# Writing the C11 quarter of a Strassen product from inside the stage that computes P2

## The chip, the cores and the metric

The kernel runs on one core of one Trainium2 chip. The metric is device time in microseconds (us) of one execution. PE is TensorE, DVE is VectorE, ACT is ScalarE, POOL is GpSimd; SP is SyncE, which here only issues transfers. "Kept" tensors lie in the chip's DRAM.

## The reference

Each token has eight experts; the output is the sum of their products, weighted by a softmax over the experts.

```python
def reference(x, router_logits, expert_weights):   # (16,512,512), (16,512,8), (8,512,2048)
    probs = exp(router_logits - max); probs = probs / sum(probs)
    for e in range(8):
        output += probs[:, :, e:e+1] * np.matmul(x, expert_weights[e])
    return output                                   # (16,512,2048) float32
```

Scaling x by the probabilities first makes this one product: 8192 tokens, an inner dimension of 8 x 512 = 4096, and 2048 output columns.

## The kernel before

**Algebra.** That product is cut into 2 x 2 blocks (tokens, experts, output columns) and done with seven products in place of eight, as Strassen and Winograd do. P1 and P2 are two of the seven, and the output block C11 is P1 + P2. Some of the seven, P1 and P2 among them, are themselves cut in the same way, with seven inner products each. `sub_product` computes one of these.

**Stages.** The program runs, in this order: an early part that sets up the probabilities and the first rows; `sub_product(1, ...)` for P1; `sub_product(5, ...)`; `sub_product(2, ...)` for P2; `sub_product(4, ...)`; and the main phase (L598 to L731), a loop over 16 groups of rows `q` that computes the remaining products and puts the output together. Stages 1, 5 and 2 store their results in `kept[r]` in DRAM; stage 4 stores straight into the output. The main phase loads P1 (`m1`) and the result of stage 5 (`m5`) back through `load_kept`, and P2 in `c11` (L588), where DVE adds P1 and the result is stored to the output.

**Inside `sub_product`** (L367). The outer loop is over `d`, eight passes. A pass loads x and probabilities (`load_x`, `load_p`), multiplies them on DVE into four z tiles (`mul`) and makes four more by additions. The inner loop is over `u`, two halves of 128 tokens. A half does seven products of eight matmuls (128 x 128 by 128 x 512) into PSUM banks named "x", "b", "q" and "d". Three products accumulate onto a bank that already holds one. ACT copies results out (`keep`, L402) and DVE combines them (`put`, L407), giving four tiles of 128 x 512 float32 per half: (group of 256 rows, column half) = (0,0), (0,1), (1,1), (1,0). `to_kept` stores them from SP. Product 1 has a bank of its own until ACT has copied it (`r1`), and `r5` and `r2` are two more such copies.

**Weights on the side.** After each pass `next(prep)` advances a generator that prepares the weights of the next stage, inside `behind()` (L125), which holds what it issues behind the last noted instruction of each engine. In P2's stage it is `weights_of_t4` (L497): after each of passes 0 to 3 it asks for a set of weight blocks (two casting loads of 512 KB, and one or two loads of 1 MB), one pass later it combines them on DVE and stores two blocks of 1 MB, and then asks for the next. `load` (L158) lets a DVE memset of two columns precede the load, so POOL's load waits for DVE.

**Queues and order.** Weight loads, casts and most output stores are issued by POOL; x, probabilities, kept tensors and weight stores by SP. Each engine works through its own instructions in order. A scheduler chooses that order beforehand, by program order and by what it reckons to be ready; `tc.keep_in_program_order` pins an instruction to program order. `dve` (L114) pins where `pinned[0]` is true, and `act` is the same function. During the four `sub_product` stages nothing is pinned, and their ACT copies are issued without `act`.

**Buffers.** Tiles of 128 x 512 float32 come from 15 slots, which `share` (L78) deals out to uses: in a new share, each use gets the slots that have been untouched longest, and `h_tile` takes the slots of a use in rotation. P2's stage has `share(xs=3, r=4, o=8)`: three for fresh x, four for ACT's copies, eight for results. PSUM has 8 banks of 128 x 512 float32, taken in rotation.

Of the kernel before, what the change touches and what calls it, by code (L numbers as in the profile page):

```python
# [32 lines left out]
def kernel(  # L33
# [7 lines left out]
    nc = tc.nc  # L41
    P = 128
    f16 = mybir.dt.float16
    f32 = mybir.dt.float32
# [8 lines left out]
    NB = 512  # L53
# [24 lines left out]
    def share(**sizes):  # L78

        order = sorted(used, key=used.get)  # L80
        for use, n in sizes.items():
            places[use], order = [order[:n], 0], order[n:]
# [24 lines left out]
    last = {}  # L107

    pinned = [True]

    def note(i):
        last[i.ins.engine] = i.ins
# [3 lines left out]
        if pinned[0]:  # L116
            tc.keep_in_program_order(i)

    act = dve

    def tt(o, a, b, op):
        dve(nc.vector.tensor_tensor(out=o, in0=a, in1=b, op=op))  # L122
# [222 lines left out]
        return z.rearrange("p e c t -> p (e c) t")  # L345


    kept = {r: [dram.tile([2, HQ, NB], f32, name=f"kept{r}_{i}") for i in range(NI)] for r in (1, 2, 5)}

    def half(use="any"):  # L350
        return h_tile([P, NB], f32, use)
# [10 lines left out]
    def from_kept(r, i, u, n, use):  # L362
        t = half(use)
        sp(t, kept[r][i][n, ds(u * P, P), :])
        return t

    def sub_product(r, odd, first, w, prep, start=0, zs=None, rest=()):  # L367

        for d in range(start, NI // 2):
            if zs:  # L370
                (a11, a12), (a21, a22) = zs
                zs = None
            else:
                hs = [4 * d + odd, 4 * d + 2 + odd]
                xp = [(load_x(h), load_p(h, first)) for h in hs]
                a11, a12 = (mul(*xp[0], e0, 2, 0, HQ) for e0 in (0, 2))
                a21, a22 = (mul(*xp[1], e0, 2, 0, HQ) for e0 in (0, 2))

            def new(a, b, op):
                z = zpool.tile([P, K8, HQ], f16, name="z", tag="z")  # L380
                tt(z, a, b, op)
                return z
            s1 = new(a21, a22, ADD)
            s2 = new(s1, a11, SUB)
            s4 = new(a12, s2, SUB)
            tt(a21, a11, a21, SUB)
            for make in rest:
                make()
            rest = ()
            z = {1: a11, 2: a12, 3: s4, 4: a22, 5: s1, 6: s2, 7: a21}  # L390

            for u in range(HQ // P):
                banks = {}

                def prod(p, b, start=True):
                    if start:
                        banks[b] = bank()
                    for k in range(K8):
                        mm(banks[b], z[p][:, k, ds(u * P, P)], w[p][:, k, :], start and k == 0, k == K8 - 1)
                    return banks[b]  # L400

                def keep(ps):  # L402
                    t = half("r")
                    nc.scalar.copy(t, ps)  # L404
                    return t

                def put(t, n, a, b, op):  # L407
                    o = half("o")
                    tt(o, a, b, op)
                    to_kept(r, 2 * d + t, u, n, o)  # L410

                r1 = keep(prod(1, "x"))
                put(0, 0, prod(2, "b"), r1, ADD)
                r5 = keep(prod(5, "q"))
                r2 = keep(prod(6, "x", False))
                put(0, 1, prod(3, "q", False), r2, ADD)
                prod(7, "x", False)
                r3 = keep(banks["x"])
                put(1, 1, banks["x"], r5, ADD)
                put(1, 0, r3, prod(4, "d"), SUB)  # L420
            with behind():
                store_x()
                next(prep, None)
        for _ in prep:
            pass
# [44 lines left out]
    def weights_of_t1():  # L470
# [5 lines left out]
            store("t1", kn, b[kn])  # L476
        yield
        ready[5] = yield from inner_weights(b)
    pinned[0] = False
    share(xs=3, r=4, o=8)  # L480
    sub_product(1, 0, P1, w, weights_of_t1(), 1,
                [[z.rearrange("p e c t -> p (e c) t") for z in zz] for zz in z1], (sums[3], sums[2]))
# [14 lines left out]
    def weights_of_t4():  # L497
# [12 lines left out]
            tt(b[kn], b[kn], t2, SUB)  # L510
        yield
        ready[4] = yield from inner_weights(b)
    share(xs=3, r=4, o=8)
    sub_product(2, 0, P2, ready[2], weights_of_t4())


    w6, w7, w3 = {}, {}, {}
# [18 lines left out]
    class Rows:  # L536
# [48 lines left out]
            self.m1[tn] = from_kept(1, self.q, *tn, "m")  # L585
            self.m5[tn] = from_kept(5, self.q, *tn, "v")

        def c11(self, j):  # L588
            tn = QUARTERS[j]
            m2 = from_kept(2, self.q, *tn, "m")  # L590
            tt(m2, self.m1[tn], m2, ADD)
            self.put(0, 0, tn, m2)

        def put(self, odd, cols, tn, o, **how):
            queue = nc.sync if self.q == NI - 1 and not how else nc.gpsimd
            queue.dma_start(out=out_rows(self.q, odd, tn[0], cols, tn[1]), in_=o, **how)  # L596
# [4 lines left out]
            make(k)  # L601
    for j in range(2):
        rows.load_kept(j)
        rows.c11(j)
    pinned[0] = True
    o10 = None
    sums = inner_weights(w3)
    for q in range(NI):
# [14 lines left out]
        for j, tn in enumerate(QUARTERS):  # L623
            if j > 1:
                rows.load_kept(j)
            x = bank()
            act(nc.scalar.copy(x, rows.m1[tn]))  # L627
            if o10 and j == 0:
                o10()
            if j > 1 or q == 1:  # L630
                rows.c11(j)
            if j < 2:
                rows.s4(j)
            else:
                ahead("a11", j - 2)
            plain(x, 6, w6, tn, False)
            v = half("u")
            tt(v, x, rows.m5[tn], ADD)
            xs.append(x)
            vs.append(v)  # L640
# [30 lines left out]
        def early(j):  # L671
            if following:
                following.load_kept(j)
                if q:
                    following.c11(j)

        ahead("s3", 0)
        if q == 0:
# [81 lines left out]
```

## Time and profile before

The median of three runs is 1435.09 us (1434.97 to 1435.35). The profiled execution has a span of 1433.2 us and a granted clock of 0.999.

| stage | from to (us) | PE busy | DVE busy | ACT busy | POOL busy | DMA share |
|---|---|---|---|---|---|---|
| early part | 0 to 42.6 | 40.6 | 26.6 | 14.9 | 12.0 | 1.03 |
| P1 | 42.6 to 211.8 | 169.2 | 123.5 | 34.0 | 17.4 | 0.98 |
| stage 5 | 211.8 to 405.2 | 193.4 | 124.7 | 37.5 | 15.2 | 0.87 |
| P2 | 405.2 to 598.6 | 193.4 | 142.3 | 37.5 | 10.4 | 0.78 |
| stage 4 | 598.6 to 792.0 | 193.4 | 132.1 | 38.8 | 13.5 | 0.70 |
| main phase | 792.0 to 1429.2 | 637.0 | 479.2 | 110.1 | 152.6 | 0.75 |

All of it is in us but the last column, the mean busy share of the 16 DMA engines, which counts the packets of two queues side by side and so can be over 1. A stage is taken to end with its last matmuls. In lines of the profile, L122 is `tt`, L142 is `mm`, L133 is `sp`, L136 is `pool`, L404 is the copy in `keep` and L596 is the output store of the main phase; a row gives an engine, an operation, what it writes and reads, its count, its busy time and the mean of one in ns, and then the idle time ahead of it with what ended that.

### The profile page before, as it was taken

What the parts mean: (1) busy time and instruction counts of PE and PEld (TensorE: products, weight loads), DVE (VectorE), ACT (ScalarE), POOL (GpSimd) and SP (SyncE); (2) the same over time, 40 slices, a digit from 0 to 9 for tenths busy, and PEclk for the clock granted to TensorE, in tenths of its full rate; (3) what the DMA queues carried; (4) which work ended last, traced back from release to release, by engine and by line L of the source; (5) the groups of instructions that cost most, each with busy time, mean ns of one, the idle gap of its engine ahead of it and who ended that gap; (6) DMA issues with size and microseconds to landing.
All of it is one profiled execution on the core that took longest, in us unless ns stands there. A gap on an engine that the chain in (4) does not pass through costs nothing.

```text
span 1433.2 us, 18192 instructions
## 1 busy us (share of the span) xinstructions
PE 1427.0 (100%) x6661; PEld 649.4 (45%) x6661; DVE 1029.0 (72%) x1171; ACT 272.8 (19%) x475; POOL 221.0 (15%) x346
## 2 busy tenths in 40 slices
PE   9999999999999999999999999999999999999998
PEld 4444444444444444444444444444444444444443
DVE  5867585647686877766767687777777877877773
ACT  3211111111111111111111211111111111111111
POOL 3111100111001000001000122222222222222220
PEclk9999999999999999999999999999999999999999
DMA  9899967799839994368865967788777777778764
GB/s 194 188 231 252 274 168 198 180 250 271 216 134 311 344 355 162 130 186 223 217 249 195 308 199 231 235 239 235 231 217 228 207 217 212 228 234 242 220 198 103
DMA packets 194329, 319.44 MB, mean 223 GB/s; under 512 B 53824, under 2 KB 83008, under 8 KB 189632
## 3 DMA queue, kind: packets, MB, share of 16 engines
q1 hardware_dynamic: 137072, 202.92, 44.7%
q0 software_dynamic: 57168, 115.37, 34.7%
q8 instruction: 52, 0.85, 0.3%
q14 instruction: 37, 0.30, 0.1%
HBM read 180.65 MB, written 159.58 MB: 237 GB/s over the span
## 4 chain that ended last, share of the span: by engine, by line
PE 94%; DMA 3%; issue 1%; POOL 1%; DVE 0%; ACT 0%; SPq 0%; POOLq 0%; DVEq 0%; ACTq 0%
PE ps L142 94%; DMA h<-kept 1%; DMA w<-in_expert_weights_dram 1%; DMA out_dram<-h 1%; POOL out_dram L596 1%; POOL w L136 0%; DVE h L122 0%; DVE z L122 0%; ACT ps L627 0%; ACT ps L646 0%; SPq L133 0%; POOL ident L235 0%; POOLq L596 0%; DVEq L122 0%; POOLq L235 0%
## 5 line engine op out<-in xcount | busy, mean ns | idle before, releaser
L142 PE MATMUL ps<-w,z 128*128 128x512 f16 x6552 | 1415.6, 379 | 0.3 <-ACT ps L627 0.2
L142 PEld LDWEIGHTS <-z 128*128 128x128 f16 x6552 | 640.9, 98 | 772.5 <-issue 0.9
L122 DVE TENSOR_TENSOR h<-ps,h 128x512 f32<-128x512 f32 x389 | 267.5, 688 | 311.2 <-PE ps L142 104.6
L122 DVE TENSOR_TENSOR z<-xT,pT 128x2048 f16<-128x2048 f16 x248 | 299.2, 1217 | 30.9 <-PE ps L142 30.9
L122 DVE TENSOR_TENSOR z<-z 128x2048 f16<-128x2048 f16 x280 | 303.5, 1107 | 7.7 <-DVE z L122 0.5
L404 ACT COPY h<-ps 128x512 f32<-128x512 f32 x248 | 145.3, 586 | 601.6 <-PE ps L142 598.3
L596 POOL DMA_DIRECT2D out_dram<-h x244 | 153.7, 664 | 533.4 <-DVE h L122 323.0
L122 DVE TENSOR_TENSOR w<-w 128x4096 f16<-128x4096 f16 x36 | 82.2, 2284 | 2.4 <-DMA w<-wdt 1.6
L663 ACT COPY h<-ps 128x512 f32<-128x512 f32 x64 | 37.4, 585 | 178.3 <-PE ps L142 175.4
L136 POOL DMA_DIRECT2D h<-in_x_dram x32 | 22.7, 709 | 283.6 <-DMA xT<-h 234.2
L122 DVE TENSOR_TENSOR h<-h 128x512 f32<-128x512 f32 (+1 forms) x67 | 46.0, 686 | 21.4 <-DMA h<-kept 21.2
L122 DVE TENSOR_TENSOR h<-h,ps 128x512 f32<-128x512 f32 x77 | 52.4, 681 | 11.4 <-PE ps L142 10.6
L136 POOL DMA_DIRECT2D w<-in_expert_weights_dram x41 | 30.7, 765 | 168.6 <-issue 77.0
L646 ACT ACTIVATE ps<-h 128x512 f32<-128x512 f32 x34 | 20.5, 602 | 160.3 <-DVE h L122 160.3
L627 ACT COPY ps<-h 128x512 f32<-128x512 f32 x64 | 35.6, 593 | 40.3 <-DMA h<-kept 31.9
L136 POOL DMA_DIRECT2D w<-wd x12 | 6.5, 542 | 188.2 <-DVE w L161 115.1
L723 ACT COPY h<-ps 128x512 f32<-128x512 f32 x15 | 8.8, 585 | 120.7 <-PE ps L142 120.7
L260 DVE CAST z<-ps 128x512 f16<-128x512 f32 x16 | 10.2, 684 | 10.4 <-PE ps L142 10.3
L712 ACT COPY h<-ps 128x512 f32<-128x512 f32 x15 | 8.8, 588 | 16.5 <-PE ps L142 16.5
L258 ACT CAST z<-ps 128x512 f16<-128x512 f32 x16 | 8.7, 589 | 16.2 <-PE ps L142 16.0
L142 PE MATMUL ps<-h,w 128*128 128x128 f16 (+1 forms) x96 | 8.5, 237 | 0.5 <-DVE lg L300 0.3
L142 PEld LDWEIGHTS <-w 128*128 128x128 f16 x96 | 6.9, 98 | 2.9 <-issue 0.7
(31 smaller groups left out, 35.0 us busy)
## 6 DMA issues: line engine op xcount, KB each, us to landing
out_dram<-h POOLq DMA_DIRECT2D x244, 256.0 KB, 5.0
kept<-h SPq DMA_DIRECT2D x192, 256.0 KB, 4.5
h<-kept SPq DMA_DIRECT2D x192, 256.0 KB, 4.8
pT<-p_dram SPq DMA_DIRECT2D x124, 256.0 KB, 5.3
w<-in_expert_weights_dram POOLq DMA_DIRECT2D x39, 512.0 KB, 12.4
out_dram<-h SPq DMA_DIRECT2D x76, 256.0 KB, 3.4
xT<-x SPq DMA_DIRECT2D x60, 256.0 KB, 3.0
w<-wd POOLq DMA_DIRECT2D x12, 1024.0 KB, 9.9
```

What stands on the lines that cost most here:

```text
L122: dve(nc.vector.tensor_tensor(out=o, in0=a, in1=b, op=op))
L136: note(nc.gpsimd.dma_start(out=o, in_=i))
L142: nc.tensor.matmul(ps, z, w, start=start, stop=stop, skip_group_check=True)
L258: act(nc.scalar.copy(o, ps))
L260: dve(nc.vector.tensor_copy(o, ps))
L404: nc.scalar.copy(t, ps)
L596: queue.dma_start(out=out_rows(self.q, odd, tn[0], cols, tn[1]), in_=o, **how)
L627: act(nc.scalar.copy(x, rows.m1[tn]))
L646: act(nc.scalar.mul(banks[b], v, scale))
L663: act(nc.scalar.copy(c21, x))
L712: act(nc.scalar.copy(r1, x))
L723: act(nc.scalar.copy(r3, x))
```

## The change

P2's stage gets the argument `prev=1`. It then loads the tiles of P1 itself, half a pass ahead (`load_prev`, four tiles per half), adds them, and stores C11 to the output from POOL. P2 is no longer kept, and the main phase has neither `c11` nor its loads. P1 is still loaded in the main phase, which needs it for the other blocks of the output.

Two of the four tiles of P1 go in by way of PSUM: `seed` has ACT copy tile (0,0) into the bank "b" of the next half and the negative of tile (1,0) into its bank "d" before PE accumulates onto them. The other two are added on DVE, which takes two additions for each of them, so that the copies `r5` and `r2` are not needed. A half thus has six additions on DVE where it had four, and two copies and two seeds on ACT where it had four copies. The four loaded tiles are updated in place and stored from there.

For this stage ACT's instructions are pinned to program order with a flag of their own, `act_pinned`, and noted as `last` of their engine. The slots are dealt out as two for x, two for copies and eleven for the tiles.

```diff
-    act = dve
+    def act(i):
+        note(i)
+        if act_pinned[0]:
+            tc.keep_in_program_order(i)
...
-    kept = {r: [... for i in range(NI)] for r in (1, 2, 5)}
+    kept = {r: [... for i in range(NI)] for r in (1, 5)}
...
+    def sub_product(r, odd, first, w, prep, start=0, zs=None, rest=(), prev=None):
+        ahead = {}
+        def load_prev(d, u):
+            ahead[d, u] = {tn: from_kept(prev, 2 * d + tn[0], u, tn[1], "o") for tn in
+                           ((0, 0), (1, 1), (0, 1), (1, 0))}
+        def seed(v):
+            banks = {"b": bank(), "d": bank()}
+            act(nc.scalar.copy(banks["b"], v[0, 0]))
+            act(nc.scalar.mul(banks["d"], v[1, 0], -1.0))
+            return banks
+        if prev:
+            load_prev(start, 0)
+            seeded = seed(ahead[start, 0])
...
-                banks = {}
+                banks = seeded if prev else {}
                 def prod(p, b, start=True):
+                    start = start and b not in banks
...
-                    nc.scalar.copy(t, ps)
+                    act(nc.scalar.copy(t, ps))
...
+                if prev:
+                    v = ahead[d, u]
+                    coming = (d, 1) if u == 0 else (d + 1, 0)
+                    if coming[0] < NI // 2:
+                        load_prev(*coming)
+                    def add(tn, a, b, op, done=True):
+                        tt(v[tn], a, b, op)
+                        if done:
+                            pool(out_rows(2 * d + tn[0], 0, u, 0, tn[1]), v[tn])
+                    r1 = keep(prod(1, "x"))
+                    add((0, 0), prod(2, "b"), r1, ADD)
+                    add((1, 1), prod(5, "q"), v[1, 1], ADD, False)
+                    add((0, 1), prod(6, "x", False), v[0, 1], ADD, False)
+                    if coming[0] < NI // 2:
+                        seeded = seed(ahead[coming])
+                    add((0, 1), prod(3, "q", False), v[0, 1], ADD)
+                    r3 = keep(prod(7, "x", False))
+                    add((1, 1), banks["x"], v[1, 1], ADD)
+                    add((1, 0), r3, prod(4, "d"), SUB)
+                    continue
...
-    share(xs=3, r=4, o=8)
-    sub_product(2, 0, P2, ready[2], weights_of_t4())
+    share(xs=2, r=2, o=11)
+    act_pinned[0] = True
+    sub_product(2, 0, P2, ready[2], weights_of_t4(), prev=1)
+    act_pinned[0] = False
...
-        def c11(self, j):
-            tn = QUARTERS[j]
-            m2 = from_kept(2, self.q, *tn, "m")
-            tt(m2, self.m1[tn], m2, ADD)
-            self.put(0, 0, tn, m2)
...
-        rows.c11(j)
...
-            if j > 1 or q == 1:
-                rows.c11(j)
...
-                if q:
-                    following.c11(j)
```

More of the change, by code (lines that the diff above doesn't have):

```diff
@@ L109 @@
     pinned = [True]
+    act_pinned = [True]
     def note(i):
@@ L345, in mul @@
         return z.rearrange("p e c t -> p (e c) t")
-    kept = {r: [dram.tile([2, HQ, NB], f32, name=f"kept{r}_{i}") for i in range(NI)] for r in (1, 2, 5)}
+    kept = {r: [dram.tile([2, HQ, NB], f32, name=f"kept{r}_{i}") for i in range(NI)] for r in (1, 5)}
     def half(use="any"):
@@ L365, in from_kept @@
         return t
-    def sub_product(r, odd, first, w, prep, start=0, zs=None, rest=()):
+    def sub_product(r, odd, first, w, prep, start=0, zs=None, rest=(), prev=None):
[11 more added lines that the diff above has]
+            seeded = seed(ahead[start, 0])
         for d in range(start, NI // 2):
@@ L478, in weights_of_t1 @@
         ready[5] = yield from inner_weights(b)
-    pinned[0] = False
+    pinned[0] = act_pinned[0] = False
     share(xs=3, r=4, o=8)
@@ L603 @@
         rows.load_kept(j)
-        rows.c11(j)
-    pinned[0] = True
+    pinned[0] = act_pinned[0] = True
     o10 = None
```

## The prediction

> **What bounds the kernel now.** I read the page's busy table first, then the waits of PE, then a table of busy time by stage, and last, for P2's stage alone, the stretches of one pass each, the DMA issues and the timeline. "Pass" is one turn of the loop over `d` in `sub_product`, "half" one turn of its inner loop over `u`.
>
> From the page, and from the answer on PE's waits:
>
> ```profile
> PE 1427.0 (100%) x6661; PEld 649.4 (45%) x6661; DVE 1029.0 (72%) x1171; ACT 272.8 (19%) x475; POOL 221.0 (15%) x346
> L142 PE MATMUL ps<-w,z 128*128 128x512 f16 x6552 | 1415.6, 379 | 0.3 <-ACT ps L627 0.2
> ```
>
> ```profile
> PE every L104 <- DVE h L101: 1.3, 1, 1.3
> PE ps L142 <- DVE lg L300: 0.3, 1, 0.3
> PE ps L142 <- DMA w<-in_x_dram: 0.2, 1, 0.2
> PE ps L142 <- ACT ps L627: 0.2, 1, 0.2
> ```
>
> The reader is to see that PE waits for nothing: three of the four waits lie in the first 15 us. A busy PE need not be PE at its peak, so I take the rate: the main phase does 2952 matmuls of 512 columns in 637.2 us (792.0 to 1429.2), 215.9 ns each, and P2's stage 896 in 193.4 us (405.2 to 598.6), 215.8 ns each. In the starts of the matmuls after 40 us there is a single gap, 582 ns at 843 us, 0.37 us too long. The change keeps every matmul. So it can save 0.4 us at most, whatever it takes off other engines; all the rest of the question is whether P2's stage can still feed PE. Here are that stage's passes 1 to 5 (times from the span's start, then busy time of PE, PEld, DVE, ACT, POOL, the clock, the DMA engines' share and GB/s):
>
> ```profile
> 429.40:453.60 24.20, 24.20 (x114) 11.00 (x113) 14.56 (x21) 4.69 (x8) 2.58 (x4) 1.00 1.01 304
> 453.60:477.70 24.10, 24.10 (x113) 10.93 (x112) 18.86 (x22) 4.69 (x8) 2.60 (x4) 1.00 1.04 321
> 477.70:501.90 24.20, 24.20 (x113) 10.94 (x112) 18.96 (x22) 4.69 (x8) 2.59 (x4) 1.00 1.07 352
> 501.90:526.10 24.20, 24.20 (x114) 11.00 (x113) 18.95 (x22) 4.69 (x8) 2.05 (x3) 1.00 1.07 359
> 526.10:550.20 24.10, 24.10 (x113) 10.92 (x112) 16.29 (x19) 4.68 (x8) 0.55 (x1) 1.00 0.78 274
> ```
>
> In four of eight passes the DMA engines are taken all the time (a share over 1 counts packets of two queues side by side), because `weights_of_t4` loads 3 MB and stores 2 MB per pass. The DMA issues of the third of them, and the timeline where the second set is asked for:
>
> ```profile
> w<-in_expert_weights_dram POOLq DMA_DIRECT2D x2, 512.0 KB, 15.9
> w<-wdt POOLq DMA_DIRECT2D x1, 1024.0 KB, 20.7
> w<-wd POOLq DMA_DIRECT2D x1, 1024.0 KB, 23.2
> ```
>
> ```profile
> 453.56 0.68 DVE L122 TENSOR_TENSOR h<-h,ps 128x512 f32<-128x512 f32 x1
> 454.15 2.28 DVE L122 TENSOR_TENSOR w<-w 128x4096 f16<-128x4096 f16 x1
> 456.39 0.07 DVE L161 MEMSET w<- 128x2 uint32 x2
> 457.01 1.51 POOL L136 DMA_DIRECT2D w<-in_expert_weights_dram  x2 [23.81 <-PE ps L142]
> 459.33 0.55 POOL L136 DMA_DIRECT2D w<-wd  x1 [0.26 <-issue]
> ```
>
> The last evacuation of a pass (453.56) frees DVE for the weights, a memset opens the gate, and POOL asks for the next set 3.4 us after that evacuation began. The four sets, from the first issue to the last landing, took 20.7, 22.5, 25.3 and 21.2 us (issues at 430.6, 457.0, 481.2, 506.1), of a pass of 24.17. DVE already waited 0.9 and 0.7 us for the third.
>
> **What the Trainium skill says.** "TensorE: Matmul & The Clock Gate", section "Wait — 56ns, not 53.3ns?", gives 215.7 ns between warm 512-column matmuls; the trace's 215.9 agrees, so PE is at its floor. "DMA: Bandwidth & Descriptors", section "Queues, rings and completion order": each queue is a ring on the same 16 engines, consumed in ring order, and the engines take turns between rings by the packet. The trace agrees as far as it goes: a 1 MB load alone in its set landed in 10.6 us (530.1), behind the casts in 18.7 to 23.2. The same page, "Anatomy of one DMA — SWDGE (gpsimd) path": engines do not wait on semaphores, the issuing sequencer does; so SP, waiting for a buffer, holds everything behind it. "PSUM — Partial Sum Buffer", section "Engine vs sequencer instructions": ScalarE's queue is strictly first in, first out; this matters for the pinned ACT order.
>
> **The change part by part.**
>
> Main phase: 64 additions on DVE go (0.68 us each, 44 us), with 64 loads and 64 stores of 256 KB. All of it lies beside a PE that never waits; worth the 0.37 us gap at 843 us, where a seed copy waited for a `kept` load. Take 0.4 us.
>
> P2's stage, DVE: six additions per half instead of four, 32 more x 0.69 = 22 us, so 142.3 becomes 164 us of 193.4. Two copies on ACT (`r5`, `r2`) go and two seeds come (0.6 us each): even. The z products for a pass are ready about 10 us before PE wants them (s1 done at 446.6, product 5 at 456.9), which hides 2.8 us per pass. Cost nothing.
>
> P2's stage, DMA: 8 `kept` stores per pass become 8 `kept` loads on the same queue, even; 8 stores of C11 on POOL's queue are new. In a light pass (550.2 to 574.4) a share of 0.39 over 24.2 us moved 12 transfers of 256 KB, 0.79 us each; 8 stores are 6.3 us of a 24.17 us pass that has nothing left.
>
> The new wait: PE's product 4 waits for bank "d", seeded by ACT from tile (1,0) of P1, the last of four loads. Buffers "o" are a ring of 11 with four taken per half, so load (1,0) for half i+1 (number 4(i+1)+3) takes the tile of number 4(i-1), tile (0,0) of half i-1, and must wait until its store landed. If i-1 is the first half of a pass, that store stands on POOL's queue behind the weight set. And there is a loop: the seed stands before `r3` in ACT's pinned order; `r3` before the last addition (1,0) of the pass on DVE; that before the weight additions and the memset; these before the next set on POOL. I work it through, time 0 at 429.4, pass n starting at 24.17(n-1), its first product 4 wanted six products (6 x 8 x 0.2158 = 10.4 us) later. Per link: set W as measured less 2 us, an estimate for SP standing still in its last third and leaving it the engines (18.7, 20.5, 23.3, 19.2); landing of the set to end of the seed: store 0.7, load 3.5 (in the main phase xT's median is 2.9, that of `kept` loads 4.8), seed 0.7, sum 4.9; then copy and addition 1.4; then 3.0 to the next issue (as 454.15 to 457.01).
> Set 1: issued 1.2, landed 19.9, seeded 24.8, last addition done 26.2.
> Set 2: issued 29.2, landed 49.7, seeded 54.6; wanted at 48.3 + 10.4 = 58.7: no stall. Addition 56.0.
> Set 3: issued 59.0, landed 82.3, seeded 87.2; wanted at 72.5 + 10.4 = 82.9: stall 4.3. Addition 88.6.
> Set 4: issued 91.6, landed 110.8, seeded 115.7; wanted at 96.7 + 4.3 + 10.4 = 111.4: stall 4.3.
> Set 5 is 1 MB: it lands 8 us sooner than a full one and the loop has caught up.
> Behind the waiting SP stand x and p loads with a lead of some 20 us; behind the waiting ACT `r1` of the next half, whose bank PE needs two halves later. No further cost. Sum 8.6 - 0.4 = +8.2 us: 1443.3.
>
> **The rivals.**
> Hidden: the loop keeps within its slack. For it: only the third and fourth links fall short, by 4 us, and each microsecond less per link takes 2 to 3 off the sum; a store (0,0) issued ahead of the set's last 1 MB would do it. Against it: all sets but one are within 4 us of a whole pass already. Time 1435.1 - 0.4 = 1434.7, not slower.
> DMA deficit: the engines, not the loop, set the pace. Shares 1.01, 1.04, 1.07, 1.07 and 0.78 plus 6.3/24.2 = 0.26 each exceed 1.07, the most seen, by 0.20 + 0.23 + 0.26 + 0.26 - 0.03 = 0.92 passes, 22 us; less the 10 us lead of z, 12 us, and with DVE waiting for weights z may come late too: 12 to 22, about 1452. Against it: kept loads alternate with weight packets at shares over 1, so part of the cost overlaps.
> Faster by more than 0.2% (2.9 us): PE leaves 0.4 us to gain, so this needs an error in the reading.
>
> **How the numbers follow.** Loop with stall 0.5 (1438 to 1450), hidden 0.27 (to 1437.9), DMA deficit 0.21, faster 0.02. Unknown costs: the load's landing from 2.9 to 4.8 us and W by 2 either way; both at their low end give no stall, both at their high end, by the same links, 22 us. Range 1434.6 to 1453.0: it takes in the hidden case and leaves out that last corner, about one in ten. Same takes the hidden case: 0.27; slower 0.71.
>
> **What would show it.** Right: PE waits on ACT seeds of 3 us or more in passes 4 and 5 of P2's stage, near 510 and 540 us; SP waiting there for stores to `out_dram`; ACT waiting for `h<-kept`; weight sets issued ever later after the end of a pass (1, 5, 11, 15 us); P2's stage near 202 us, main still 637. DMA share up in passes 1 to 5. Wrong: all passes 24.17 us long (hidden); DVE waiting for weights and PE for z (deficit); a stall in pass 0, where no weights load; or a main phase longer than before.

## The result, and the profile after

The changed kernel takes 1459.45 us (median of four runs, 1458.92 to 1460.26) against 1435.03 us for the kernel before in the same runs: a ratio of 1.0171, with a 95% interval of 1.0153 to 1.0188. It is 24.4 us slower. The forecast was 1443.3 us with a range to 1453.0: the direction was right, the size three times too small.

Where the time went is read from the starts of the matmuls, stage by stage. P2's stage grew from 193.4 to 217.2 us. Stage 4 stayed at 193.4 us. The main phase went from 637.3 to 636.9 us. So nearly all of the loss, 23.8 us, lies in the stage that was changed. From the page of after, and from its answer on the waits of PE (us in total, times, longest):

```profile
PE 1434.3 (98%) x6661; PEld 650.4 (45%) x6661; DVE 1009.1 (69%) x1139; ACT 270.0 (19%) x475; POOL 223.3 (15%) x350
L146 PE MATMUL ps<-w,z 128*128 128x512 f16 x6552 | 1423.3, 380 | 16.8 <-DVE h L126 14.8
L383 ACT ACTIVATE ps<-h 128x512 f32<-128x512 f32 x16 | 9.6, 602 | 63.9 <-DMA h<-kept 61.1
```

```profile
PE ps L146 <- DVE h L126: 14.8, 5, 5.2
PE every L104 <- DVE h L101: 1.3, 1, 1.3
PE ps L146 <- DMA w<-in_expert_weights_dram: 0.8, 2, 0.7
PE ps L146 <- ACT h L425: 0.8, 1, 0.8
```

PE, which had waited for nothing, now waits 14.8 us for DVE, in five pieces. L126 is `tt`, L146 is `mm`, L383 is the seed of bank "d", L425 the copy in `keep`, and L140 is `pool`. The seed's row has the mark that was forecast: ACT stood idle for 61.1 us in all until a tile of P1 had landed. But PE's row isn't the one forecast: the engine that PE waits for is DVE, and not ACT with its seeds. The passes 1 to 6 (start and end, length, busy time of PE, PEld, DVE, ACT and POOL, granted clock, DMA share, GB/s):

```profile
430.00:454.40 24.40, 24.36 (x114) 10.96 (x113) 16.60 (x23) 3.44 (x6) 6.94 (x12) 1.00 1.01 316
454.40:485.60 31.20, 27.15 (x113) 11.54 (x112) 21.23 (x25) 4.45 (x8) 6.94 (x12) 0.89 1.06 358
485.60:517.60 32.00, 26.03 (x113) 11.26 (x112) 21.23 (x25) 4.45 (x8) 6.95 (x12) 0.95 0.99 327
517.60:548.40 30.80, 25.82 (x113) 11.27 (x112) 21.22 (x24) 4.97 (x9) 6.45 (x11) 0.94 1.02 334
548.40:573.50 25.10, 24.52 (x113) 10.96 (x112) 19.42 (x23) 5.32 (x10) 4.87 (x9) 1.00 0.99 363
573.50:597.90 24.40, 24.36 (x114) 10.93 (x113) 19.03 (x22) 4.38 (x8) 4.32 (x8) 1.00 0.67 230
```

Three passes carry it. They last 31.2, 32.0 and 30.8 us in place of 24.17, and in the same three the clock is below 1.00. Share times length over passes 1 to 5 is 145.7 us of full DMA, where the five stretches of before give 120.1: 25.6 us more work for the same engines. The forecast's rival took 6.3 us a pass, 31.5 us in five, and found 22 of them to be more than the engines had left.

The mechanism is in the timeline from the second set of weights to the third (start, length, engine, line, what is written and read, idle time before it and what ended that). These are the lines that follow one from another:

```profile
463.12 1.53 POOL L140 DMA_DIRECT2D w<-in_expert_weights_dram  x2 [1.96 <-issue]
...
465.94 0.55 POOL L140 DMA_DIRECT2D out_dram<-h  x1
...
486.26 0.32 SPq L137 DMA_DIRECT2D h<-kept  x1
...
490.06 0.60 ACT L383 ACTIVATE ps<-h 128x512 f32<-128x512 f32 x1 [13.73 <-DMA h<-kept]
490.60 1.06 ACT L425 COPY h<-ps 128x512 f32<-128x512 f32 x2
491.21 0.69 DVE L126 TENSOR_TENSOR h<-ps,h 128x512 f32<-128x512 f32 x1 [6.02 <-ACT h L425]
...
492.95 0.68 DVE L126 TENSOR_TENSOR h<-h,ps 128x512 f32<-128x512 f32 x1
...
493.55 2.28 DVE L126 TENSOR_TENSOR w<-w 128x4096 f16<-128x4096 f16 x1
...
495.86 2.29 DVE L126 TENSOR_TENSOR w<-w 128x4096 f16<-128x4096 f16 x1
496.42 1.52 POOL L140 DMA_DIRECT2D w<-in_expert_weights_dram  x2 [1.96 <-issue]
...
498.08 0.68 DVE L126 TENSOR_TENSOR h<-ps,h 128x512 f32<-128x512 f32 x1
...
498.69 1.28 DVE L126 TENSOR_TENSOR h<-ps,h 128x512 f32<-128x512 f32 x2
...
499.42 1.01 PE L146 MATMUL ps<-w,z 128*128 128x512 f16 x2 [5.17 <-DVE h L126]
```

Its DMA issues at the head of that stretch (size, us from issue to landing):

```profile
w<-in_expert_weights_dram POOLq DMA_DIRECT2D x2, 512.0 KB, 13.2
w<-wdt POOLq DMA_DIRECT2D x1, 1024.0 KB, 18.5
w<-wd POOLq DMA_DIRECT2D x1, 1024.0 KB, 20.2
out_dram<-h POOLq DMA_DIRECT2D x1, 256.0 KB, 20.3
```

This is the loop of the prediction. A store of C11 issued at 465.94 lands 20.3 us later, right after the weights ahead of it on POOL's queue (465.4 + 20.2 = 485.6, and 486.2). SP waits for its slot and at once asks for the tile of P1; ACT seeds the bank 3.8 us after that; `r3` follows, then DVE's last addition (492.95), the two weight additions, and the third set is asked for at 496.42.

The end of the chain is what the prediction didn't have. PE is at product 3 there, which accumulates onto bank "q", and DVE must first have read "q" for tile (1,1). That is the first of the two additions at 498.69 (the one at 498.08 is for tile (0,0)); it ends at 499.37, and PE resumes at 499.42. In before it was ACT that read "q" (`r5`) and "x" (`r2`). In after DVE does, and in its order that reading stands behind the last addition of the pass before, two weight additions of 2.3 us and the addition for tile (0,0). The three large stalls, 4.0 us (ending at 466.1), 5.2 us (at 499.4) and 4.9 us (at 530.3), are all of this kind.

The clock adds to each of them. Two stretches of 2.0 and 3.6 us after the stall that ended at 499.4:

```profile
499.40:501.40 2.00, 1.98 (x5) 0.69 (x5) 1.70 (x2) 0.00 (x0) 0.22 (x1) 0.50 1.06 165
...
505.40:509.00 3.60, 3.60 (x18) 1.62 (x17) 2.24 (x3) 1.08 (x2) 1.08 (x2) 1.00 1.08 348
```

At a clock of 0.50 five matmuls start in 2 us, then sixteen in 3.6 us (x18 also counts those that had begun before). The clock record has three stretches at 0.50 in this stage, of 6.8, 3.4 and 3.4 us, of which 2.6 us lie inside the stalls: (13.65 - 2.6) / 2 = 5.5 us of PE's work is lost to them. The Trainium skill, "TensorE: Matmul & The Clock Gate", section "What's actually happening", says that the clock halves after an idle window of about 3.4 us and that the window runs freely; the lengths 3.4 and twice 3.4 agree. That PE must be idle for a whole window does not agree: in a later run a stall of 2.7 us was followed by half clock too.

Over the whole stage, the starts of the matmuls come 23.85 us late in sum: about 17 us in stalls, and most of the rest at the halved clock.

### The profile page after: what moved, and what is told of

It reads as the page before. It is cut to its first block, busy times and chain, and to the rows that moved or that the text cites. A ratio compares the mean times of both kernels' runs of the same rounds, so it can differ in the third digit from the quotient of the medians.

```text
span 1457.7 us, 17859 instructions
## 1 busy us (share of the span) xinstructions
PE 1434.3 (98%) x6661; PEld 650.4 (45%) x6661; DVE 1009.1 (69%) x1139; ACT 270.0 (19%) x475; POOL 223.3 (15%) x350
## 4 chain that ended last, share of the span: by engine, by line
PE 90%; DMA 4%; issue 3%; DVE 2%; POOL 1%; SPq 0%; ACT 0%; DVEq 0%; POOLq 0%; ACTq 0%
PE ps L146 90%; DMA out_dram<-h 3%; DMA w<-in_expert_weights_dram 1%; DVE h L126 1%; DVE w L126 1%; DVE z L126 0%; DMA pT<-p_dram 0%; POOL w L140 0%; POOL out_dram L140 0%; DMA h<-kept 0%; SPq L137 0%; ACT h L425 0%; DVEq L126 0%; POOL ident L239 0%; POOLq L140 0%
## 5 line engine op out<-in xcount | busy, mean ns | idle before, releaser
L146 PE MATMUL ps<-w,z 128*128 128x512 f16 x6552 | 1423.3, 380 | 16.8 <-DVE h L126 14.8
L146 PEld LDWEIGHTS <-z 128*128 128x128 f16 x6552 | 642.1, 98 | 795.6 <-issue 28.1
L126 DVE TENSOR_TENSOR h<-ps,h 128x512 f32<-128x512 f32 x421 | 288.7, 688 | 381.0 <-PE ps L146 145.7
L126 DVE TENSOR_TENSOR z<-xT,pT 128x2048 f16<-128x2048 f16 x248 | 299.8, 1216 | 30.8 <-PE ps L146 30.5
L126 DVE TENSOR_TENSOR z<-z 128x2048 f16<-128x2048 f16 x280 | 304.0, 1106 | 6.5
L425 ACT COPY h<-ps 128x512 f32<-128x512 f32 x216 | 126.1, 585 | 548.5 <-PE ps L146 514.6
L126 DVE TENSOR_TENSOR w<-w 128x4096 f16<-128x4096 f16 x36 | 82.2, 2283 | 0.1
L699 ACT COPY h<-ps 128x512 f32<-128x512 f32 x64 | 37.4, 585 | 179.3 <-PE ps L146 176.4
L140 POOL DMA_DIRECT2D h<-in_x_dram x32 | 22.7, 709 | 296.4 <-DMA xT<-h 243.5
L140 POOL DMA_DIRECT2D out_dram<-h x64 | 34.8, 544 | 198.1 <-DVE h L126 192.3
L126 DVE TENSOR_TENSOR h<-h,ps 128x512 f32<-128x512 f32 x77 | 52.4, 680 | 9.8 <-PE ps L146 9.5
L682 ACT ACTIVATE ps<-h 128x512 f32<-128x512 f32 x34 | 20.5, 602 | 200.3 <-DVE h L126 200.3
L140 POOL DMA_DIRECT2D w<-in_expert_weights_dram x41 | 30.9, 768 | 36.4 <-DVE w L165 22.3
L665 ACT COPY ps<-h 128x512 f32<-128x512 f32 x64 | 34.5, 593 | 0.0
L757 ACT COPY h<-ps 128x512 f32<-128x512 f32 x15 | 8.8, 585 | 120.7 <-PE ps L146 120.7
L140 POOL DMA_DIRECT2D w<-wd x12 | 6.5, 543 | 154.1 <-PE ps L146 128.9
L383 ACT ACTIVATE ps<-h 128x512 f32<-128x512 f32 x16 | 9.6, 602 | 63.9 <-DMA h<-kept 61.1
L264 DVE CAST z<-ps 128x512 f16<-128x512 f32 x16 | 10.2, 684 | 12.7 <-PE ps L146 12.7
L382 ACT COPY ps<-h 128x512 f32<-128x512 f32 x16 | 9.5, 594 | 14.7 <-DMA h<-kept 14.6
L746 ACT COPY h<-ps 128x512 f32<-128x512 f32 x15 | 8.8, 585 | 16.5 <-PE ps L146 16.5
```

Source lines behind the costliest of these rows:

```text
L140: note(nc.gpsimd.dma_start(out=o, in_=i))
L146: nc.tensor.matmul(ps, z, w, start=start, stop=stop, skip_group_check=True)
L264: dve(nc.vector.tensor_copy(o, ps))
L382: act(nc.scalar.copy(banks["b"], v[0, 0]))
L383: act(nc.scalar.mul(banks["d"], v[1, 0], -1.0))
L425: act(nc.scalar.copy(t, ps))
```

## The experiments

The expectations weigh two theories. The loop: the store behind the weights holds a slot, the slot holds the load, the load holds the seed, and the seed holds DVE and the next set. The deficit: the stores of C11 are 25 us more of DMA work, and PE must wait until it is done, whatever the order. Every time below has the kernel before beside it in the same runs, at 1434.6 to 1435.2 us. Twelve of the eighteen results lie in none of the ranges that were stated for them: six fall between the ranges and six above them all. So neither theory alone is right. A table of the main numbers comes after the experiments.

### One link of the loop at a time, all bytes kept

**A larger ring.** One slot moves from x to the tiles, so that load (1,0) no longer takes the tile whose store stands behind the weights.

```diff
-    share(xs=2, r=2, o=11)
+    share(xs=1, r=2, o=12)
```

> Only the slots differ: 12 for the tiles of P1 instead of 11, one for fresh x instead of two, so that the load of tile (1,0) for the next half takes the tile of the last store of two halves ago, which was issued ahead of the weight set, and no longer that of the first store of the half before, which stands behind it. Theory of the loop (load (1,0) waits for that store, the seed for the load, r3 for the seed, DVE for r3): the wait goes, 1434 to 1439 us. Rival of the DMA deficit (all bytes are still moved): within 3 us of 1459. Rival of DVE (two more additions per half, and banks now read by DVE): within 3 us of 1459.

Measured: 1453.38 us, ratio 1.0131 (1.0102 to 1.0161). It takes 6 us off, a quarter, and lands above the loop's range and below its rivals'; P2's stage is still 212.6 us. SP's waits in the stage (total, times, longest), for this kernel:

```profile
SPq L137 <- DMA out_dram<-h: 83.0, 35, 7.9
SPq L137 <- DMA w<-in_expert_weights_dram: 35.8, 4, 10.8
```

In after the first of these was 107.2 us. A new one takes part of its place: SP now stands at a weight store, waiting for a set to land, with loads of P1 behind it. One more slot moves the knot rather than undoing it.

**The loads in another order.**

```diff
-                           ((0, 0), (1, 1), (0, 1), (1, 0))}
+                           ((1, 0), (0, 0), (1, 1), (0, 1))}
```

> Only the order of the four loads differs: (1,0) first, (0,1) last, so that the load that has to wait for the store behind the weights is one that DVE wants in product 6 of the next half, not one that ACT seeds from. SP still waits as long. Theory of the loop: ACT is not held up, r3 and the weights come on time; some waiting remains where tile (0,1) comes late for DVE: 1435 to 1446 us. DMA deficit: within 3 us of 1459. DVE: within 3 us of 1459.

Measured: 1463.35 us, ratio 1.0201 (1.0159 to 1.0243): not better, probably worse, and outside both ranges. The tile that comes late is now (0,1), and DVE stands at its addition for 24.0 us in three waits (longest 11.0), with all of its other work behind it; PE waits 23.2 us for DVE. A late tile costs through the queue it stops, whichever tile it is.

**The seeds after `r3`.** ACT's order is changed so that a late tile holds up no copy of the pass that is ending.

```diff
-                    if coming[0] < NI // 2:
-                        seeded = seed(ahead[coming])
                     add((0, 1), prod(3, "q", False), v[0, 1], ADD)
                     r3 = keep(prod(7, "x", False))
+                    if coming[0] < NI // 2:
+                        seeded = seed(ahead[coming])
```

> Only ACT's order differs: the two seeds of the next half stand behind r3. Theory of the loop: the late tile now holds up r1 of the next half instead of r3; the last addition of a pass and the weights come on time, so the loop is cut, 1435 to 1446 us. DMA deficit: within 3 us of 1459. DVE: within 3 us of 1459.

Measured: 1452.41 us, ratio 1.0125 (1.0095 to 1.0154), 7 us off, again between the ranges. PE's waits for DVE shrink to 0.8 us; instead it waits 10.9 us for ACT's copies (longest 7.5). That is `r1` of the next half, which now stands behind the waiting seeds, and product 6, the fourth of a half, needs its bank.

**The copies back on ACT.** `r5` and `r2` are made again, so that DVE's order frees no bank. They need a third slot, which comes from x.

```diff
-                    add((1, 1), prod(5, "q"), v[1, 1], ADD, False)
-                    add((0, 1), prod(6, "x", False), v[0, 1], ADD, False)
+                    add((1, 1), keep(prod(5, "q")), v[1, 1], ADD, False)
+                    add((0, 1), keep(prod(6, "x", False)), v[0, 1], ADD, False)
...
-    share(xs=2, r=2, o=11)
+    share(xs=1, r=3, o=11)
```

> The copies r5 and r2 on ACT are put back (slots: one for x, three for copies, eleven for the tiles), so that PE's products 3 and 7 wait for ACT's reading of the banks and not for DVE's; loads, stores, ring and seeds are as in the changed kernel, so the late tile is as late. If what costs is that DVE, late and with two weight additions of 2.3 us ahead, has become the reader of bank q: PE's waits for DVE go and what is left is a wait for ACT behind the seed, 1437 to 1449 us. If it is the lateness of the seed alone, whoever reads the bank: 1452 to 1460. DMA deficit: within 3 us of 1459.

Measured: 1453.15 us, ratio 1.013 (1.01 to 1.0159). The waits of PE, whole:

```profile
PE ps L146 <- ACT h L425: 13.5, 3, 7.9
```

The wait for DVE is gone and three waits for ACT's copies stand in its place. So the DVE order that ended the chain in after is one outlet of the loop and not its cause: with that outlet shut, it comes out at the copies behind the waiting seed.

### Stores on another queue

If the store's place behind the weights is the trouble, another issuer should help. SP was tried, then ACT, and then ACT together with the edit of the copies above; the expectations follow in that order.

```diff
-                            pool(out_rows(2 * d + tn[0], 0, u, 0, tn[1]), v[tn])
+                            sp(out_rows(2 * d + tn[0], 0, u, 0, tn[1]), v[tn])
```

> The changed kernel with its 64 stores of C11 issued by SP instead of POOL; PE, DVE and ACT have the same instructions in the same order, and the same bytes move, but no store stands behind a weight set on POOL's queue. Theory of the loop: the wait for the store behind the weights goes, 1435 to 1443 us. DMA deficit (the bytes of passes 1 to 5 take longer than the passes): 1449 to 1460.

```diff
-                            pool(out_rows(2 * d + tn[0], 0, u, 0, tn[1]), v[tn])
+                            act(nc.scalar.dma_start(out=out_rows(2 * d + tn[0], 0, u, 0, tn[1]), in_=v[tn]))
```

> The changed kernel with C11's stores issued by ACT, pinned where they stand in the program, so that they have a DMA ring of their own: behind no weight set, and no kept load waits behind them on SP. The bytes are the same. If what costs is that the slots of the tiles come free only after a weight set: 1436 to 1443 us, with SP's waits for out_dram mostly gone. If the sum of the bytes and the near deadline of the loads costs, whatever the ring: 1450 to 1462.

> As store_act, with the copies r5 and r2 back on ACT (slots 1, 3, 11). Without a late slot the only other cost seen, some 0.3 us per pass where PE waits for DVE to read a bank, goes as well: 1434 to 1439 us. If bytes and deadline cost: 1449 to 1460.

Measured: 1478.24 us from SP (ratio 1.03, 1.027 to 1.033), 1469.17 from ACT (1.0238), 1471.39 from ACT with the copies (1.0254): all worse, and above every range. From SP, a store waits for DVE's result, and loads of P1 stand behind it; SP's waits for landed stores did not shrink either (118.1 us in the stage, 107.2 in after). From ACT the experiment brought in a wait of its own, seen in the timelines of ACT and SP of the first of the two:

```profile
446.25 0.34 ACTq L437 DMA_DIRECT2D out_dram<-h  x1
446.58 0.32 SPq L137 DMA_DIRECT2D h<-kept  x1
454.17 0.34 ACTq L437 DMA_DIRECT2D out_dram<-h  x1
454.60 0.59 ACT L425 COPY h<-ps 128x512 f32<-128x512 f32 x1 [9.45 <-DMA h<-kept]
```

The issues themselves take 0.34 us each. Between them ACT stands until 454.09, when the load that SP had asked for at 446.58 lands: in this program that load and the store of 454.17 report their landing by the same semaphore, and the store is not issued before the semaphore is free. A copy of a product waited behind it, and PE for the copy. So these three don't separate the two theories: each new queue brought waits of its own. How much of their loss is due to which wait isn't shown.

### Bytes taken away, and bytes added

**No stores of C11.** The line that stores is replaced by `pass`.

> The changed kernel without the 64 stores of C11 (a block of the output stays unwritten); PE, DVE and ACT have the same instructions in the same order. Both the loop and the DMA deficit hang on these stores: 1434 to 1437 us. If the seeds, the pinned order of ACT or the additions on DVE cost anything by themselves, it stays: over 1440.

Measured: 1438.03 us over 15 runs, ratio 1.0022 (1.0014 to 1.003). The loss falls from 24.4 to 3.1 us. Loads of P1, seeds, ACT's pinned order and 32 more additions are all still there. That is what both theories have in common: without the stores neither loop nor deficit is left.

**No stores, and the copies back on ACT** (this and the edit of the copies together).

> The changed kernel without the 64 stores of C11 (a block of the output stays unwritten) and with the copies r5 and r2 back on ACT. The changed kernel without the stores alone took 1438.0. If its 3 us over the kernel before are PE waiting for DVE to read banks x and q: 1434.5 to 1435.5. If they are the seeds or ACT's pinned order: 1437 to 1439.

Measured: 1435.83 us over 10 runs, ratio 1.0007 (0.9997 to 1.0017); P2's stage is 193.39 us long, as in before. So the seeds, the pinned order and the added DVE work cost nothing measurable, and 1438.0 - 1435.8 = 2.2 us is the price of having DVE, not ACT, read "q" and "x". In the kernel without stores these are waits of PE of under 0.4 us, one or two in every pass (24.38 to 24.72 us long in place of 24.17), where it accumulates onto a bank that DVE has yet to read.

**The same bytes in the kernel before, without seeds and loads of P1.** Each result of P2 is stored a second time, to a tensor that nothing reads. Before then moves as many 256 KB blocks per pass as after: 8 kept stores and 8 more.

```diff
+                if r == 2:
+                    sp(twice[i][n, ds(u * P, P), :], t)
```

> The kernel before, in which P2's stage stores each of its 64 result tiles twice, from SP, to two places in DRAM: 2 MB more per pass, as the change has, but no seeds, no loads of P1 and nothing on POOL's queue behind the weights. DMA deficit: passes 1 to 5 of P2's stage become too long for their bytes, 1445 to 1458 us. Theory of the loop: 1434 to 1438.

Measured: 1436.66 us over 10 runs, ratio 1.0014 (1.0004 to 1.0024). Its passes 5 to 7, in the columns of the table of passes:

```profile
526.20:550.40 24.20, 22.51 (x105) 10.15 (x104) 17.56 (x19) 4.00 (x7) 0.55 (x1) 1.00 1.04 394
550.40:574.50 24.10, 24.10 (x114) 10.96 (x112) 21.07 (x22) 4.69 (x8) 0.00 (x0) 1.00 1.02 388
574.50:598.60 24.10, 24.10 (x114) 10.86 (x113) 18.79 (x19) 4.69 (x8) 0.00 (x0) 1.00 0.83 305
```

The DMA engines are full two passes longer than in before, and PE lost 1.7 us in one of them (22.51 of 24.2 us busy). The backlog was carried into the light passes. So a deficit of this size isn't by itself a loss; it becomes one where the work that is late is work that PE needs soon.

**The second store from POOL instead**, behind the weights.

```diff
+                if r == 2:
+                    pool(twice[i][n, ds(u * P, P), :], t)
```

> The kernel before, whose 64 results of P2 are stored a second time by POOL, so behind the weight sets; no seeds and no loads of P1. The slots of the results, eight, four per half, then come free as late as the changed kernel's. If a late slot alone is enough: DVE waits for stores and PE for DVE or ACT, 1440 to 1452 us. If a seed that waits for a load is needed too: 1435 to 1438, as when SP stored them twice (1436.7).

Measured: 1440.22 us over 5 runs, ratio 1.004 (1.0024 to 1.0056): 3.6 us dearer than the same bytes from SP. A place behind the weights costs something even where no load waits for the slot.

**Four weight stores of 1 MB left out** of P2's stage (the blocks are cast again later).

```diff
-            store(22, kn, t)
```

> The changed kernel without the four stores of 1 MB of weight blocks of expert group 22 in P2's stage; stage 4 and the main phase cast those blocks from the expert weights again. C11's stores stand behind the weight sets as before. DMA deficit: 4 x 2.5 us of engine time less (1 MB at the 24.5 to 26.5 GB/s per engine that its packets have), so 8 to 12 us faster than the changed kernel, 1447 to 1452. Theory of the loop: the weight sets land 1 to 2 us sooner each, 2 to 6 us faster, 1453 to 1458.

Measured: 1454.92 us, ratio 1.0138 (1.0108 to 1.0167): 4.5 us off for 4 MB less. Bytes count, but 1 MB per pass, half of what the change stores in those four passes, taken off elsewhere buys only a fifth of the loss.

### The bytes small, the chain kept

Each store of C11 is issued as before, but covers only the first 256, or the first 64, of its 512 columns. Slots, queues and order stay; the bytes nearly go.

```diff
-                            pool(out_rows(2 * d + tn[0], 0, u, 0, tn[1]), v[tn])
+                            pool(out_rows(2 * d + tn[0], 0, u, 0, tn[1])[:, 0:64], v[tn][:, 0:64])
```

> The changed kernel, whose stores of C11 write only the first 256 of 512 columns of each tile (half of the block stays unwritten). Instructions, waits and order on PE, DVE, ACT and POOL are the same; 1 MB less per pass. If the bytes of these stores cost (no stores 1438, all 1459.5): 1442 to 1450. If their place behind the weight sets and the waits for them cost: 1454 to 1460.

> As store_half, with the first 64 columns only. If the bytes cost: 1438 to 1442. If the place behind the weights and the waits cost: 1452 to 1460.

Measured: 1452.11 us with 256 columns, 1449.87 with 64 (ratio 1.0103, 1.0074 to 1.0132), both between their ranges. With an eighth of the bytes, 14.8 of the 24.4 us remain. The DMA issues and then PE's timeline of the kernel with 64 columns:

```profile
w<-wd POOLq DMA_DIRECT2D x1, 1024.0 KB, 19.0
out_dram<-h POOLq DMA_DIRECT2D x1, 32.0 KB, 18.7
```

```profile
424.69 58.76 PE L146 MATMUL ps<-w,z 128*128 128x512 f16 x268
484.61 2.53 PE L146 MATMUL ps<-w,z 128*128 128x512 f16 x11 [1.16 <-ACT h L425]
492.32 26.63 PE L146 MATMUL ps<-w,z 128*128 128x512 f16 x112 [5.18 <-DVE h L126]
520.85 9.44 PE L146 MATMUL ps<-w,z 128*128 128x512 f16 x43 [1.90 <-DVE h L126]
```

A store of 32 KB landed 18.7 us after its issue, with the weights that had been asked for ahead of it. For its landing the size hardly matters; the place does. The Trainium skill, "DMA: Bandwidth & Descriptors", section "Queues, rings and completion order", says, in a paragraph on the queues of SP and ACT, that an engine takes the descriptors of one ring in their order; POOL's queue here agrees. The chain then ends in the same 5.2 us stall.

**The chain loosened at two links, bytes small.** The ring of 12 and the seeds after `r3`, together with the stores of 64 columns.

> The changed kernel with 12 slots for the tiles (one for fresh x) and the seeds behind r3, and stores of C11 of the first 64 columns only (the rest of the block stays unwritten); PE, DVE and POOL have the order of store_eighth. If the half of the cost that remains at an eighth of the bytes is the loop: it goes, 1437 to 1441 us, as without stores. If it is something else: 1446 to 1451, as store_eighth.

Measured: 1439.31 us over 7 runs, ratio 1.0028 (1.0016 to 1.0041). The loop's cost, at small bytes, is thereby taken out by changes of order and slots alone: 1449.9 - 1439.3 = 10.6 us.

**The same two edits, all bytes.**

> The same two edits with all bytes. If the loop and the bytes add: 1446 to 1450. If the bytes cost only by way of the loop: 1437 to 1442. If the loop is not it: within 3 us of the single edits, 1450 to 1456.

Measured: 1450.54 us, ratio 1.0108 (1.0078 to 1.0137). PE's timeline around its stalls:

```profile
487.37 26.22 PE L146 MATMUL ps<-w,z 128*128 128x512 f16 x112 [2.73 <-ACT h L425]
517.20 12.98 PE L146 MATMUL ps<-w,z 128*128 128x512 f16 x47 [3.61 <-ACT h L425]
```

With the loop loosened, the other seven eighths of the bytes cost 1450.5 - 1439.3 = 11.2 us. Taken by itself this result fits "the loop is not it": it lies in that range, 0.5 us above the one for a sum, and 2 to 3 us below the single edits. What speaks for the loop is the pair: the same two edits take off 10.6 us at small bytes and nearly as much, 1459.5 - 1450.5 = 9.0 us, at full bytes. Nor is the loop gone here: PE's waits are now for `r1`, behind late seeds. The clock record has 10.2 us at half speed. This is the best version of the change that was found; it doesn't reach the kernel before.

**Three edits.** The copies on ACT, the seeds after `r3`, and twelve slots for tiles; there is then no slot of its own left for x, which shares the tiles' slots. It was run also without the four weight stores.

```diff
-    share(xs=2, r=2, o=11)
+    share(r=3, o=12)
```

> The changed kernel with 12 slots for the tiles, the seeds behind r3 and the copies r5 and r2 on ACT, all bytes kept. If the loop's single links each gave way to the next when one was cut: 1435 to 1442. If the bytes cost, because a tile's slot ties each load to a store of two or three halves ago and a backlog of the DMA engines can't be carried over to the light passes: 1446 to 1456.

> three_edits without the four 1 MB stores of weight blocks in P2's stage (cast again later). If the loop: as three_edits, 1435 to 1442. If the bytes: 6 to 10 us below three_edits.

Measured: 1469.40 us (ratio 1.0239) and 1465.04 (1.0209). The waits of PE in the first:

```profile
PE ps L146 <- DVE z L126: 22.0, 2, 11.5
PE ps L146 <- ACT h L425: 4.4, 2, 3.5
```

Fresh x had to wait for a tile's store, and z came 22 us late. That is a cost of the sharing and hides what the three edits do for the loop; what all three would give with slots enough stays open.

### The loop's pace in the kernels

The loop can be seen at one place, the times at which POOL asks for the four sets. The last column is the time over before of the same runs.

| kernel | sets asked for at (us) | first to fourth | over before |
|---|---|---|---|
| before | 430.6, 457.0, 481.2, 506.1 | 75.5 | |
| no C11 stores | 432.3, 458.9, 483.4, 507.7 | 75.4 | 3.1 |
| two edits, 64 columns | 432.1, 458.8, 483.9, 507.5 | 75.4 | 4.2 |
| two edits | 432.8, 459.5, 486.9, 514.6 | 81.8 | 15.4 |
| 64 columns | 432.0, 458.3, 489.3, 517.6 | 85.6 | 14.8 |
| seeds after `r3` | 432.7, 459.0, 485.5, 518.3 | 85.6 | 17.8 |
| ring of 12 | 432.5, 459.1, 492.9, 518.8 | 86.3 | 18.8 |
| 256 columns | 432.5, 458.8, 491.8, 521.1 | 88.6 | 17.0 |
| copies back on ACT | 432.1, 461.8, 495.2, 525.6 | 93.5 | 18.6 |
| after | 432.8, 463.1, 496.4, 527.0 | 94.3 | 24.4 |

Where the sets keep the pace that they have in before, at most 4.2 us are lost. In after, three turns of the loop take 94.3 us, and the three long passes together 94.0 us: PE runs at the loop's pace. What is lost beyond the slip of the sets is small waits, half clock and later passes. The slip isn't the loss itself: in the kernel before with its second store from POOL the sets slip as far as with the two edits (82.5 us from first to fourth), and only 5.3 us are lost.

## Why the prediction was right in direction and wrong in size

**PE at its floor, 0.4 us to gain.** Right. The gap at 843 us is gone, and the main phase is 0.4 us shorter.

**DVE's 22 us, the two seeds and the pinned order at nothing.** Right for the work itself: without stores and with the copies on ACT, the stage is as long as before. Wrong by 2.2 us in one respect that wasn't priced: moving the reading of "q" and "x" from ACT to DVE put DVE's order onto PE's path.

**The links of the loop.** Right in kind, and near in size. Sets 1 to 4 took 17.5, 22.5, 20.2 and 17.0 us (taken: 18.7, 20.5, 23.3, 19.2). From the landing of sets 1 to 3 to the end of the seed it was 7.1, 5.1 and 4.9 us (taken: 4.9), and then 5.8, 5.8 and 5.5 us to the next issue (taken: 4.4). From one issue to the next, 30.3, 33.3 and 30.6 us were measured and 28.0, 29.8 and 32.6 taken: 94.3 against 90.4 in sum. The first pass has no stall, as forecast. The waits of SP for stores and of ACT for tiles of P1 came as forecast, the longest 13.5 and 13.7 us.

**The slack between the loop and PE.** This is the step of the mechanism that failed: "Behind the waiting SP stand x and p loads with a lead of some 20 us; behind the waiting ACT `r1` of the next half, whose bank PE needs two halves later. No further cost." With it goes the deadline "10.4 us later", at PE's product 4. By that deadline the loop would have cost nothing: the late seeds of tile (1,0) were done 3.0, 5.1 and 3.9 us after the three long passes began. What stands behind the waiting seed is needed much sooner. Bank "x", which `r1` must leave, is accumulated onto by product 6 of the same half, the fourth of seven: three products, 5.2 us, after the pass begins. Bank "q" is accumulated onto by product 3, the fifth, but DVE's reading of it stands behind the last addition and both weight additions, 4.6 us. The large stalls of after are of the second kind, those of the kernels with the copies back or the seeds later are of the first, and none is at product 4. The forecast had two stalls, in passes 4 and 5; there were three, in passes 2, 3 and 4. I took 8.6 us for the loop; 10.6 us were measured at an eighth of the bytes, where the sets slip 10.1 us. That these sums are so near is partly luck, since the place, the number and the cause of the stalls were other than forecast.

**The deficit as a rival of the loop.** This failed too, as a matter of adding up, and it is the larger part of the missing time. The forecast gave the loop nothing for the extra bytes (it took its sets as 2 us shorter than those of before) and gave the deficit a chance of its own, in place of the loop. The runs show both in the same kernel: 10.6 us of loop and then 1459.5 - 1449.9 = 9.6 us for the other seven eighths of the bytes, or 11.2 us where the loop is loosened. The added DMA work, 25.6 us, was four fifths of the 31.5 us taken; that the 10 us lead of z hides a part of it wasn't tested. That less than half of it shows agrees with the second store in before, which cost 1.7 us because its backlog could wait for light passes. In after it can't: the loads of P1 lead by half a pass, and a ring of eleven slots ties each to an earlier store.

**What was left out.** PE runs at half clock after its stalls: 5.5 us in after, within the sums above.

The 24.4 us divide as follows, each part the difference of two neighbours in one chain of kernels (so that they add up by construction): 0.8 us left with neither stores nor DVE's readings, 2.2 us for those readings, 1.3 us that the two edits leave at small bytes, 10.6 us for the loop, 9.6 us for the bytes. The loop and the bytes aren't independent: stores grown from one eighth to a half cost 2.2 us (1449.9 to 1452.1), and from a half to the whole 7.3 us. How the bytes' share divides between longer sets, later tiles and later x isn't settled; a kernel with all bytes and so many slots that no load waits for a store would tell, and wasn't tried.

## What to carry to other kernels

Where a load reuses a buffer whose store is queued behind bulk transfers, the load was late by the whole bulk here, whatever the store's size; follow what then stands behind the waiting instruction on each engine to the first thing that PE needs, and take the earliest such deadline, not that of the tile itself. A PSUM bank that PE accumulates onto again must be read by an engine whose order holds nothing slow, and moving the read to another engine brings that engine's whole queue onto PE's path. Two causes that need the same slack add up: in these runs extra DMA work in a full stage cost 1.7 us where it could be late, and almost half of its 25.6 us once it sat inside a loop that PE waits for.

## What the runs showed of the hardware that was not expected

- A store of 32 KB took 18.7 us to land behind 3 MB of weights on the same queue, about as long as a store of 256 KB in the same place (20.3 us).
- Issuing a store took ACT's queue 0.34 us (median of 64). The Trainium skill, "DMA: Bandwidth & Descriptors", section "Issuing engines are not separate DMA queues", calls the sequencer's time for an issue usually small beside the transfer, and this agrees. What held ACT for 7.5 us was the landing of another engine's load whose semaphore the store was to use.
- The three stalls of 4.0 to 5.2 us in after were each followed by 3.4 or 6.8 us at half the clock, with matmuls starting 427 ns apart in place of 216. In the kernel with two edits so were stalls of 2.7 and 3.6 us, the first about 1 us after PE had resumed; in the one with 64 columns besides, whose longest was 1.4 us, the clock stayed at 1.00. So it did after a stall of 2.8 us in the kernel without the four weight stores: of two stalls of nearly one length, one was followed by half clock and the other was not.
